# q and gate columns of the second pair of blocks by Strassen's algorithm, in a stage of their own

## Chip, cores, metric

One Trainium2 chip, one core. The time is the device time of one execution in microseconds (us), as a median of runs; beside it stands one profiled execution with its trace. TensorE (PE) multiplies, VectorE (DVE), ScalarE (ACT) and GpSimd (POOL) do the rest, SyncE (SP) issues most of the DMAs.

## The reference

One layer of a hybrid decoder on a prompt of 2048 tokens and 8 x 4 sample tokens (32 rows), width 1024:

```
h = rmsnorm(x); z = h @ w_in
hq, hf, hi, hg, sq, sk, sv, ga, gb = split(z)   # 512, 512, 512, 512, 512, 128, 128, 1024, 1024 columns
y_a = (rmsnorm(gated linear recurrence of hq, f(hf), hi) * silu(hg)) @ w_up_a
y_b = (sliding-window attention of rotary(sq), rotary(sk), sv, with sinks) @ w_up_b
m = sigmoid(ga) * y_a + sigmoid(gb) * y_b
x = x + m @ w_o
x = x + square(relu(rmsnorm(x) @ w_ff1)) @ w_ff2       # inner width 4096
y = rmsnorm(x)
```

The new state of the recurrence and the last window of keys and values are outputs as well.

## The kernel before

The prompt is cut into four blocks of 512 tokens (`bi` 0 to 3); the 32 sample rows join the last, which has T = 544. Two blocks make a pair (`sb` 0 and 1). A pair goes through its two blocks one after the other, up to the output projection `w_o`, and then both together through the MLP. Matrix products of float32 data are made of three passes in fp32r: each operand is split into a high part (ACT cast) and a low part (DVE subtraction), and high x high, high x low and low x high are added up in PSUM (`split_out`, `split_in`, `split_w`).

In a block all activations lie transposed as two operands `hT` (k tiles 0 to 3 and 4 to 7; slots 0 and 1 of seven large SBUF slots `op(0)` to `op(6)`, which every stage reuses). The order in the program: value columns hi (`colN512`), the pending norms of the block before (`late`), q columns hq (`colT`, four tiles of 128 columns), attention columns sq and skv, the attention over four chunks (`swa_scores`, `swa_values`), hf, the levels of the recurrence with hg in between (`hgrn_levels`), the outputs of the recurrence (`hgrn_out`, `hgrn_tail`), then eight tiles of gate gb with w_up_b and eight of gate ga with w_up_a (`gate`), then `w_o`. In `gate` a tile of the gate (8 k x 3 matmuls) goes through tanh on ACT, the up-projection (4 k x 3) into another PSUM bank, and DVE multiplies them; for ga POOL adds the other branch, and the sum is split into `mT`. A tile of 512 tokens is one matmul wide, in the last block two (288 and 256, `segs`).

The MLP is Strassen's algorithm already, in Winograd's form with seven products. The two blocks of the pair are the two halves of the token axis (Th = 512 or 528 each), the k tiles 0 to 3 and 4 to 7 the two halves of the inner axis, and two column tiles of w_ff1 the two halves of the columns: tile n is paired with tile n + 16. Sums of activations (S1 to S4) are made once, sums of weights (T1 to T4) for each pair of tiles (`Wpair`); in the second pair of blocks the 528 tokens go in two chunks of 264. `Unit` makes the seven products of a pair and chunk: `a` the two that need only unsummed operands (B11 A11, B21 A12), `b` three (T2 S2, T1 S1, T3 S3), `c` two (T4 A22, B22 S4). Of each PSUM bank a copy is taken between products (`snap`). The first six or ten units run their `a` ahead. The results and their sums go to DRAM (`us`, seven stores per unit) and are the operands of the second product (`f2`), which gathers its result in `yacc` in SBUF. While it runs for the first pair, block 2's activations are normalised and transposed (`load_T_parts`); block 3's during block 2's `w_o`. Then `Fin` transposes `yacc` back, adds the residual, normalises and stores.

The program is unrolled, and the Tile framework's planner sets the order on each engine at build time: it takes what its own cost model says is ready, with program order as priority. So a matmul group later in the program runs earlier where another waits. Waits between engines are semaphores. Tiles of a pool take turns in `bufs` buffers; a pool that is opened after another is closed takes the same memory, and its tiles wait for the old tiles that they overlap (`reuse_waits="tile"`).

Of the kernel before, what the change touches and what calls it, by code (L numbers as in the profile page):

```python
# [7 lines left out]
F32 = mybir.dt.float32  # L8
# [8 lines left out]
P = 128  # L17
# [26 lines left out]
def tile_hybrid_step(  # L44
# [188 lines left out]

    def geometry(bi):
# [16 lines left out]
    def load_T_parts(bi, i, hT, xt, on_dve=False, sm=None, junk=None, hwf=None):  # L251
        kind, r0, nr, c = geometry(bi)[5][i]
        src = xs if kind == "s" else xp[bi * bt + c * P:bi * bt + (c + 1) * P, :]
        N = f"ab{bi}{c}"
        x = []

        def pre():
            x.append(xt())
            nc.sync.dma_start(x[0][0:nr, :], src)
            norm_pre(x[0], x[0], nr, N, on_dve, sm, junk and junk())  # L260

        def out(half, tp, wb):
            hw = (hwf or t2)(f"hw_{N}_{half}")[:, 0:512].rearrange("p (k t) -> p k t", k=4)[:, :, 0:nr]
            nc.vector.tensor_tensor(hw, tp, wb, ALU.mult)
            split_out(hT[half][:, 0, :, r0:r0 + nr], hT[half][:, 1, :, r0:r0 + nr], hw)

        return pre, lambda: norm_post(x[0], nr, n1c, N, out)

    wk_ctx = ExitStack()
    wk = wk_ctx.enter_context(tc.tile_pool(name="wk0", bufs=1, reuse_waits="tile"))  # L270
    hT_next = start_T(0)
    x_first = op(6, F32, "x_first")
    for i in range(ncb):
        for part in load_T_parts(0, i, hT_next, lambda: x_first[:, i * D:(i + 1) * D], on_dve=True):
            part()
# [26 lines left out]
    def w2_sums(i):  # L302
        tt = nc.vector.tensor_tensor
        r = {}
        for kh in range(2):
            for nh in range(2):
                r[kh, nh] = wk.tile([P, 512], F32, tag="ws", bufs=5, name=f"ws{i}{kh}{nh}")
                nc.sync.dma_start(r[kh, nh], w2[(kh * NP + i) * P:(kh * NP + i + 1) * P, nh * 512:(nh + 1) * 512])
        t3 = wk.tile([P, 512], F32, tag="ws", bufs=5, name=f"ws{i}t")
# [4 lines left out]
        for o, x in (("T3", t3), ("T1", r[0, 1]), ("T2", r[1, 1]), ("T4", r[1, 0])):  # L314
            nc.sync.dma_start(wT[o][i * P:(i + 1) * P, :], x)

    late = []
    x1 = [tc.dram_tile([geometry(bi)[2], D], F32, name=f"x1_{bi}") for bi in range(nblk)]
    for bi in range(nblk):
# [28 lines left out]
        s1W = W1[:, 2 * n4:2 * n4 + 8 * NS].rearrange("p (x h t) -> p x h t", x=2, h=HH)
        qS, kS, fS, aS = s0W[:, 0], s0W[:, 1], s1W[:, 0], s1W[:, 1]
        SV = op(4, F32, "SV_" + B)  # L350
        qT = SV[:, 0:4 * T].rearrange("p (g t) -> p g t", g=G)
        vN = SV[:, 4 * TM:4 * TM + 512 * ncb].rearrange("p (c e) -> p c e", e=512)
        if smp:
            vS = wk.tile([NS, 512], F32, tag="vS", name="vS")
# [28 lines left out]
        def colN(c0, name, fn):  # L383
# [7 lines left out]
        def colN512(c0, name, fn):  # L391
            rings = [mm_ps, mm_ps, hg_ps, hg_ps, sw_ps]
            ps = [rings[i](f"ps_{name}_{t[3]}") for i, t in enumerate(tiles)]
            gemm_NK(w_in, c0, [(p, t[1], t[2]) for p, t in zip(ps, tiles)], h_acts, name)
# [81 lines left out]
        colN512(C_HI, f"hi{B}", ev_v)  # L476
        while late:
            norm_post(*late.pop(0))

        for h in range(HH):  # L480
            colT(C_HQ, h, f"hq{B}{h}", ev_q)
        qkv = op(5, F32, "qkv_" + B)[:, 0:len(tiles) * 768].rearrange("p (c e) -> p c e", e=768)

        def ev_sq(ps, kind, c, nr):
            ti = c if kind == "p" else ncb
            nc.scalar.activation(
                qkv[0:nr, ti, 0:512].rearrange("p (g v d) -> p v g d", g=G, v=NKV),
                ps.rearrange("p (v g d) -> p v g d", g=G, v=NKV), AF.Copy, scale=HD ** -0.5)
# [5 lines left out]
        colN512(C_SQ, f"sq{B}", ev_sq)  # L494
        colN(C_SQ + 512, f"skv{B}", ev_skv)

# [171 lines left out]

        for h in range(HH):
            colT(C_HF, h, f"hf{B}{h}", ev_f)  # L670

# [10 lines left out]
        while gens:  # L682
            gens = [g for g in gens if next(g, None) is not None]
            if rnd in hg_at:
# [88 lines left out]

        b_acts = [(ob[:, 0, k, :], ob[:, 1, k, :]) for k in range(4)]
        pb = op(5, F32, "pb_" + B)[:, 0:KD * T].rearrange("p (k t) -> p k t", k=KD)

        def gate(c0, j, uu, acts, dst, z):
            js = slice((j % 2) * P, (j % 2 + 1) * P)
            gu = unit_rows(w_in, 0, KD, c0 + j * P, P, f"g{z}{B}{j}")
            for (t0, n) in segs:  # L780
                N = f"{z}{B}{j}_{t0}"
                o = dst(j, t0, n)
                ps = mm_ps("g" + N)
                gemm_T(ps, n, [(gu[0][:, k, :], gu[1][:, k, :]) for k in range(KD)], h_acts, t0)
                nc.scalar.activation(o, ps[:, 0:n], AF.Tanh, scale=0.5)
                ps = sw_ps("y" + N)
# [4 lines left out]
        for j in range(KD):  # L791
# [6 lines left out]
            if sb == 0 and j % 2 == 1:  # L798
                w2_sums(8 * bi + j // 2)
# [7 lines left out]
        for j in range(KD):  # L807
            if sb == 0 and j % 2 == 1:
                w2_sums(8 * bi + 4 + j // 2)
            if j % 2 == 0:  # L810
                ua = unit_rows(w_ua, 0, 4, j * P, 256, f"ua{B}{j}")
            for t0, n, o in gate(C_GA, j, ua, a_acts, lambda j, t0, n: t2(f"ta_{B}{j}_{t0}")[:, 0:n], "a"):
# [27 lines left out]
        tt = nc.vector.tensor_tensor  # L840
# [65 lines left out]
        if odd:  # L906
            rings = (sw_ps, sw_ps, hg_ps, hg_ps, mm_ps)
# [14 lines left out]
        else:  # L922
            ntl = geometry(bi + 1)[5]
            loads = [load_T_parts(bi + 1, i, hT_next, lambda i=i: t4(f"x_b{bi + 1}_{i}")) for i in range(len(ntl))]
            todo = []
            for i in range(len(ntl) + 1):
                if i < len(ntl):
                    todo.append(loads[i][0])
                if i > 0:
                    todo.append(loads[i - 1][1])  # L930
# [7 lines left out]
            for cg in range(2):  # L938
                rings = ((sw_ps, sw_ps, hg_ps, hg_ps), (mm_ps, mm_ps, sw_ps, sw_ps))[cg]
# [9 lines left out]
        chunks = [(0, Th)] if Th <= 512 else [(0, Th // 2), (Th // 2, Th // 2)]  # L949
# [4 lines left out]

        def prod(ps, wv, av, k0, t0, n, first, last=True):
            for k in range(4):
                wh, wl = wv[:, 0, k, k0:k0 + P], wv[:, 1, k, k0:k0 + P]
                ah, al = av[:, 0, k, t0:t0 + n], av[:, 1, k, t0:t0 + n]
# [387 lines left out]
```

## Time and profile before

| | |
|---|---|
| median of 3 runs | 2934.21 us (2930.34 to 2935.71) |
| profiled execution | 2930.84 us, span of its instructions 2929.1 us |
| granted TensorE clock, mean | 0.992 |
| PE busy | 2841.5 us, 97% |
| weight loads (PEld) busy | 2453.5 us, 84% |
| DVE / ACT / POOL busy | 1629.4 / 1136.1 / 215.0 us |
| HBM read / written | 334.07 / 107.64 MB |

Matmuls are pipelined, so their durations overlap: what one costs is read from how many a stretch holds, not from its mean duration. The pair 0 of blocks ends near 1399 us of the span, block 2 at 1770, block 3 at 2229, the first MLP product of the second pair at 2584.

### The profile page before, as it was taken

The page shows a single profiled execution, that of the slowest core. Times are in us where ns is not written, and L with a number is a line of the kernel's source. Part 1 is how long each engine was busy: PE and PEld are TensorE (multiplying, and loading weights), DVE is VectorE, ACT ScalarE, POOL GpSimd, SP SyncE. Part 2 cuts the span into 40 slices and gives each one's busy share as a digit, 9 for nine tenths or more (in the row PEclk, how much of TensorE's full clock was granted, in tenths as well). Part 3 has the DMA queues.
Part 4 walks back from the last instruction along what each step waited for, and adds up shares of the span by engine and source line. Part 5 has one row for each costly group of instructions (what it writes and reads, how often), then busy time and mean ns, then how long its engine had stood idle before and what let it go on. Part 6 is the DMA issues. An engine that isn't in the chain of part 4 may idle for free.

```text
span 2929.1 us, 49035 instructions
## 1 busy us (share of the span) xinstructions
PE 2841.5 (97%) x19967; PEld 2453.5 (84%) x19967; DVE 1629.4 (56%) x2559; ACT 1136.1 (39%) x2093; POOL 215.0 (7%) x360
## 2 busy tenths in 40 slices
PE   7999999999899999999999999999998999999998
PEld 6778877788778888887777888878997999999998
DVE  5674434734777674454456343275347777754446
ACT  3443334423433344442354233333234333344433
POOL 0110111101200000000111011100003000000001
PEclk9999999999999999999999999999999999999999
DMA  7746342145654465565422434212346454485553
GB/s 251 238 154 219 105 144 66 45 122 158 197 165 155 159 232 206 196 214 173 151 64 68 125 115 135 62 52 84 116 133 197 151 157 140 146 304 179 186 195 104
DMA packets 410539, 443.92 MB, mean 152 GB/s; under 512 B 22588, under 2 KB 290840, under 8 KB 410296
## 3 DMA queue, kind: packets, MB, share of 16 engines
q1 hardware_dynamic: 402160, 413.48, 44.0%
q0 software_dynamic: 5600, 18.70, 2.1%
q10 hardware_dynamic: 2552, 8.60, 0.8%
q8 instruction: 157, 2.57, 0.4%
q14 instruction: 70, 0.57, 0.1%
HBM read 334.07 MB, written 107.64 MB: 151 GB/s over the span
## 4 chain that ended last, share of the span: by engine, by line
PE 43%; DMA 3%; DVE 2%; ACT 1%; issue 1%; POOL 1%; SPq 0%; POOLq 0%; DVEq 0%; ACTq 0%
PE f L1180 3%; PE f L1179 3%; PE f L1181 3%; PE fB L959 2%; PE fB L961 2%; PE fB L960 2%; PE gab L169 1%; PE gab L170 1%; PE gab L168 1%; PE gbb L170 1%; PE gbb L169 1%; PE gbb L168 1%; PE fD L959 1%; PE fD L961 1%; PE fD L960 1%
## 5 line engine op out<-in xcount | busy, mean ns | idle before, releaser
L1179 PE MATMUL f<-f2S,hw2T 128*128 128x264 f32 (+1 forms) x576 | 183.7, 319 | 0.0
L1180 PE MATMUL f<-f2S,hw2T 128*128 128x264 f32 (+1 forms) x576 | 183.6, 319 | 0.0
L1181 PE MATMUL f<-f2S,lw2T 128*128 128x264 f32 (+1 forms) x576 | 183.5, 319 | 0.0
L155 DVE TENSOR_TENSOR lw2T<-lw2T,hw2T 128x1024 fp32r<-128x1024 f32 x64 | 78.1, 1224 | 106.0 <-ACT hw2T L154 105.5
L959 PE MATMUL fB<-S,w1T 128*128 128x264 f32 (+1 forms) x384 | 124.2, 325 | 7.3 <-DVE c L1027 3.7
L1180 PE MATMUL f<-f2A,h_w2B 128*128 128x264 f32 (+1 forms) x384 | 122.5, 319 | 1.4 <-DVE f2A L155 1.4
L961 PE MATMUL fB<-S,w1T 128*128 128x264 f32 (+1 forms) x384 | 123.4, 322 | 0.0
L1179 PE MATMUL f<-f2A,h_w2B 128*128 128x264 f32 (+1 forms) x384 | 122.6, 319 | 0.8 <-ACT f2A L154 0.8
L960 PE MATMUL fB<-S,w1T 128*128 128x264 f32 (+1 forms) x384 | 123.3, 322 | 0.0
L1181 PE MATMUL f<-f2A,l_w2B 128*128 128x264 f32 (+1 forms) x384 | 122.2, 319 | 0.0
L154 ACT CAST hw2T<-lw2T 128x1024 fp32r<-128x1024 f32 x64 | 67.3, 1052 | 126.6 <-DMA lw2T<-w_T 114.3
L1180 PEld LDWEIGHTS f<-f2S,hw2T 128*128 128x128 f32 x576 | 108.4, 188 | 7.4
L1179 PEld LDWEIGHTS f<-f2S,hw2T 128*128 128x128 f32 x576 | 108.4, 188 | 7.4
L1181 PEld LDWEIGHTS f<-f2S,lw2T 128*128 128x128 f32 x576 | 108.0, 188 | 7.5
L169 PE MATMUL gbb<-hT_b,h_gbb 128*128 128x512 f32 (+2 forms) x320 | 113.2, 354 | 0.0
L168 PE MATMUL gbb<-hT_b,h_gbb 128*128 128x512 f32 (+2 forms) x320 | 113.1, 353 | 0.0
L170 PE MATMUL gbb<-hT_b,l_gbb 128*128 128x512 f32 (+2 forms) x320 | 112.9, 353 | 0.0
L169 PE MATMUL gab<-hT_b,h_gab 128*128 128x512 f32 (+2 forms) x320 | 111.7, 349 | 0.0
L170 PE MATMUL gab<-hT_b,l_gab 128*128 128x512 f32 (+2 forms) x320 | 111.6, 349 | 0.0
L168 PE MATMUL gab<-hT_b,h_gab 128*128 128x512 f32 (+2 forms) x320 | 111.4, 348 | 0.0
L155 DVE TENSOR_TENSOR f2S<-f2S 128x1024 fp32r<-128x1024 f32 (+1 forms) x64 | 79.4, 1242 | 51.9 <-ACT f2S L154 50.3
L231 DVE TENSOR_TENSOR l_w2B<-rw2B,h_w2B 128x1024 fp32r<-128x1024 f32 x48 | 58.8, 1225 | 81.1 <-ACT h_w2B L230 74.7
(717 smaller groups left out, 8821.1 us busy)
## 6 DMA issues: line engine op xcount, KB each, us to landing
w1r<-w_ff SPq DMA_DIRECT2D x150, 256.0 KB
lw2T<-w_T SPq DMA_DIRECT2D x64, 512.0 KB
rw2B<-w_ff SPq DMA_DIRECT2D x48, 512.0 KB
u_S<-s SPq DMA_DIRECT2D x128, 132.0 KB
f2S<-u_S SPq DMA_DIRECT2D x32, 528.0 KB
ws<-w_ff SPq DMA_DIRECT2D x64, 256.0 KB
r_gbb<-w_in SPq DMA_DIRECT2D x32, 512.0 KB
r_gab<-w_in SPq DMA_DIRECT2D x32, 512.0 KB
```

Source lines behind the costliest of these rows:

```text
L154: nc.scalar.copy(hi, F(lo))
L155: nc.vector.tensor_tensor(lo, F(lo), F(hi), ALU.subtract)
L168: nc.tensor.matmul(ps[:, 0:n], wh, rh, start=(k == 0), stop=False)
L169: nc.tensor.matmul(ps[:, 0:n], wh, rl, start=False, stop=False)
L170: nc.tensor.matmul(ps[:, 0:n], wl, rh, start=False, stop=(k == nk - 1))
L231: nc.vector.tensor_tensor(dl, src, F(dh), ALU.subtract)
L959: nc.tensor.matmul(ps, wh, ah, start=(first and k == 0), stop=False, skip_group_check=not first)
L960: nc.tensor.matmul(ps, wh, al, start=False, stop=False, skip_group_check=not first)
L961: nc.tensor.matmul(ps, wl, ah, start=False, stop=(last and k == 3), skip_group_check=not first)
L1179: nc.tensor.matmul(ps, wh, ah, start=first, stop=False, skip_group_check=cont)
L1180: nc.tensor.matmul(ps, wh, al, start=False, stop=False, skip_group_check=cont)
L1181: nc.tensor.matmul(ps, wl, ah, start=False, stop=lastk, skip_group_check=cont)
```

## The change

For the second pair of blocks (`zs`, sb > 0) the columns hq, gb and ga leave the blocks: 4 + 8 + 8 = 20 column tiles (NZ) become 10 pairs of neighbouring tiles, and a stage ahead of block 2 makes them for both blocks at once with the same seven products (`strassen_T`, now a function shared with the MLP).

- During the first pair's second MLP product all nine token tiles of the second pair are normalised (`norm_tile`), not four; the raw result goes to DRAM (`hraw`) by POOL's queue, and block 2's half is split into `hT` (528 tokens: 512 and 16 sample rows).
- Between the pairs: attention columns skv and sq of block 2, stored to DRAM (`zqk`); the four raw quarters come back by POOL's queue into tiles of a pool `zq` (14 buffers, 6 per k); `op_sums` makes S1 to S4 and A22 from them in slots 2 to 6.
- The stage runs in a pool `zp` opened after `zq` is closed. `z_fin` takes tanh of the gates on ACT and stores to DRAM (`zd`) from ACT's queue, the q tiles from POOL's.
- Block 2 reads q, k, v and both blocks read q (`qW`) and the gates (`pb`, `ga`) back by POOL's queue. `gate` is left with the up-projection. hi moves behind the attention. Block 3's activations are reloaded from `hraw` (`reload`) during block 2's `w_o`.
- In the MLP tile 2n is paired with 2n + 1, so that two loads of 256 columns take the place of four of 128; the weight sums are made in the loaded tiles; T4 is split later (`late`); T3 and T4 have buffers of their own (`we`); the result tiles have 12 buffers per chunk, not 16; the seven stores of a unit go by POOL's queue, not SP's. w_ff2 is read in the permuted order.
- In the first pair `w_o` uses other PSUM rings, and the normalised rows go to DRAM through `t4` tiles.

```diff
+    class Wpair:
+        def done(u, name, raw):
+            v = (u.wt if name in ("T3", "T4") else wtile)(F32R, ...)
+            split_out(v[:, 0], v[:, 1], raw)
+        def early(u):
+            v = wtile(F32, f"w1r0_{u.N}").rearrange("p (s k c) -> p s k c", s=2, k=4)
+            for kh in range(2):
+                nc.sync.dma_start(v[:, kh], u.src(u.n, kh)[:, 0:P].rearrange("(k p) c -> p k c", p=P))
+                u.done(f"B{kh + 1}1", v[:, kh])
+        def rest(u):
+            for kh in range(2):
+                v = wtile(F32, f"w1r{kh + 1}_{u.N}").rearrange("p (k c) -> p k c", k=4)
+                nc.sync.dma_start(v, u.src(u.n, kh).rearrange("(k p) c -> p k c", p=P))
+                b += [v[:, :, 0:P], v[:, :, P:2 * P]]
...
+            tt(b11, b12, b11, ALU.subtract)
+            tt(b12, b22, b12, ALU.subtract)
+            u.done("B22", b22)
+            tt(b22, b22, b11, ALU.subtract)
+            tt(b21, b21, b22, ALU.subtract)
+            u.done("T2", b22)
+            u.done("T1", b11)
+            u.done("T3", b12)
...
+    def strassen_T(N, npairs, src, chunks, A, st, fin, ahead, wt, hook=None):
...
+        for i in range(ahead):
+            if i % nch == 0:
+                units[i].pair.early()
+            units[i].a(i < 4)
+        for i, u in enumerate(units):
+            if i % nch == 0:
+                u.pair.rest()
+            if i >= ahead:
+                u.a()
+            if i:
+                units[i - 1].c()
+            if i % nch == 0:
+                u.pair.late()
+            u.b()
+        units[-1].c()
...
+                if raw:
+                    nc.gpsimd.dma_start(hraw[b][oo][...], hw[:, :, s:s + n])
+                if oo == tgt:
+                    split_out(hT[half][:, 0, :, d:d + n], hT[half][:, 1, :, d:d + n], hw[:, :, s:s + n])
...
+    def op_sums(A, sl, a11, a12, a21, a22, s1, s2):
+        tt(s1, a21, a22, ALU.add)
+        tt(s2, s1, a11, ALU.subtract)
+        tt(a11, a11, a21, ALU.subtract)
+        tt(a12, a12, s2, ALU.subtract)
+        for n, x in (("S2", s2), ("S1", s1), ("S3", a11), ("A22", a22), ("S4", a12)):
+            split_out(sl(A[n], 0), sl(A[n], 1), x)
...
+        if zs and not odd:
+            colN(C_SQ + 512, f"skv{B}", st_skv)
+            colN512(C_SQ, f"sq{B}", st_sq)
+            for k in range(4):
+                z = {n: zq.tile([P, Th], F32, tag="zs", bufs=14, ...) for n in ("a11", "a12", "a21", "a22", "s1", "s2")}
+                for n, o, g in (("a21", 1, 0), ("a22", 1, 1), ("a11", 0, 0), ("a12", 0, 1)):
+                    nc.gpsimd.dma_start(z[n], hraw[sb][o][(4 * g + k) * P:(4 * g + k + 1) * P, :])
+                op_sums(A, lambda v, i: v[:, i, k], *(...))
+            zq_ctx.close()
+            with tc.tile_pool(name=f"zp{sb}", bufs=1, reuse_waits="tile") as zp:
+                def z_fin(u, blk, x, ps=None):
+                    if zi >= HH:
+                        nc.scalar.activation(x, x if ps is None else ps, AF.Tanh, scale=0.5)
+                    q = nc.scalar if zi >= HH else nc.gpsimd
+                    if o == 0:
+                        q.dma_start(zd[bi][rs, c0:min(c1, bt)], x[:, 0:min(c1, bt) - c0])
+                        if c1 > bt:
+                            q.dma_start(zd[bi + 1][rs, 0:c1 - bt], x[:, bt - c0:u.ln])
+                    else:
+                        q.dma_start(zd[bi + 1][rs, o2 + c0:o2 + c1], x)
+                def z_st(ln, name):
+                    return zp.tile([P, ln], F32, tag="st", bufs=(16 if len(chunks) == 1 else 15), name=name)
+                strassen_T(f"z{sb}", NZ // 2, z_src, chunks, A, z_st, z_fin, 6 if len(chunks) == 1 else 10, ...)
...
+            if not zs:
+                gu = unit_rows(w_in, 0, KD, c0 + j * P, P, f"g{z}{B}{j}")
-                ps = sw_ps("y" + N)
+                ps = (sw_ps, mm_ps)[(j + i) % 2 if zs else 0](f"y{z}{B}{j}_{t0}")
...
+                s1, s2, s3, s4 = u.st("s1"), u.st("s2"), u.c21, u.st("s4")
-                        nc.sync.dma_start(us[o][u.n // 4][...], x)
+                    nc.gpsimd.dma_start(us[o][u.n // 4][...], y_)
-                    return fp.tile([P, u.ln], F32, tag="st", bufs=16 * len(chunks), ...)
+                       lambda ln, name: fp.tile([P, ln], F32, tag="st", bufs=12 * len(chunks), name=name),
```

More of the change, by code (lines that the diff above doesn't have):

```diff
@@ L231, in split_out, with prod @@
         nc.vector.tensor_tensor(dl, src, F(dh), ALU.subtract)
+    def prod(ps, wv, av, k0, t0, n, first, last=True):
+        for k in range(4):
+            wh, wl = wv[:, 0, k, k0:k0 + P], wv[:, 1, k, k0:k0 + P]
+            ah, al = av[:, 0, k, t0:t0 + n], av[:, 1, k, t0:t0 + n]
+            nc.tensor.matmul(ps, wh, ah, start=(first and k == 0), stop=False, skip_group_check=not first)
+            nc.tensor.matmul(ps, wh, al, start=False, stop=False, skip_group_check=not first)
+            nc.tensor.matmul(ps, wl, ah, start=False, stop=(last and k == 3), skip_group_check=not first)
@@ new lines, in strassen_T @@
+    def strassen_T(N, npairs, src, chunks, A, st, fin, ahead, wt, hook=None):
+        ws = [Wpair(N, n, src, wt) for n in range(npairs)]
+        nch = len(chunks)
+        units = [Unit(i, ws[i // nch], *chunks[i % nch], A, st, fin) for i in range(npairs * nch)]
+        for i in range(ahead):
[12 more added lines that the diff above has]
+            u.b()
+            if hook is not None:
+                hook()
+        units[-1].c()
@@ L269, in tile_hybrid_step, with hw_w @@
+        return [pre, lambda: norm_post(x[0], nr, n1c, N, out)]
+    hT_next = [opT(0, g, "hT") for g in range(2)]
+    x_first = op(6, F32, "x_first")
     wk_ctx = ExitStack()
     wk = wk_ctx.enter_context(tc.tile_pool(name="wk0", bufs=1, reuse_waits="tile"))
[L271 to L274, printed above, removed]
+    def hw_w(name):
+        x = wtile(F32, name)
+        return x, lambda half: x[:, half * 512:(half + 1) * 512]
@@ new lines, in hw_t2, with z_ops @@
+    def hw_t2(name):
+        return None, lambda half: t2(f"{name}{half}")
+    def z_ops(b):
+        return {n: opT(b, slot, "z" + n) for n, slot in (("S1", 4), ("S2", 5), ("S3", 3), ("A22", 2), ("S4", 6))}
+    def op_sums(A, sl, a11, a12, a21, a22, s1, s2):
[5 more added lines that the diff above has]
+            split_out(sl(A[n], 0), sl(A[n], 1), x)
@@ L275, in tile_hybrid_step @@
+    for (o, c) in tiles_of(0)[:ncb]:
+        for part in norm_tile(0, (o, c), hT_next, lambda: x_first[:, c * D:(c + 1) * D], small, hw_t2, True, raw=False):
             part()
@@ L474, in ev_v, with qk_in, qk_out @@
             nc.scalar.copy(vS if kind == "s" else vN[:, c, :], ps)
[L476 to L482, printed above, removed]
+        def qk_in(ps):
+            return ps.rearrange("p (v g d) -> p v g d", g=G, v=NKV)
+        def qk_out(x):
+            return x.rearrange("p (g v d) -> p v g d", g=G, v=NKV)
@@ L953, in tile_hybrid_step @@
         us = {o: [tc.dram_tile([4 * P, Th], F32, name=f"u_{o}_{g}_{sb}") for g in range(KG)] for o in OPS}
[L955 to L958, printed above, removed]
-                nc.tensor.matmul(ps, wh, ah, start=(first and k == 0), stop=False, skip_group_check=not first)
-                nc.tensor.matmul(ps, wh, al, start=False, stop=False, skip_group_check=not first)
-                nc.tensor.matmul(ps, wl, ah, start=False, stop=(last and k == 3), skip_group_check=not first)
         with tc.tile_pool(name=f"f1_{sb}", bufs=1, reuse_waits="tile") as fp:
@@ L1215, in tile_hybrid_step @@
                                 evac(si, j, t0, ln, banks[j][ci])
-                    if not last and 1 <= si <= ncb and g in (1, 2):
-                        loads[si - 1][g - 1]()
+                    if not last and si >= 1 and todo:
+                        todo.pop(0)()
             nj = op(6, F32, f"nj{sb}")
```

418 lines of the change are left out of this document (238 added, 180 removed).

## The prediction

> **What bounds the kernel now.** I read the page first: the span, busy times, and the chain that ended last.
>
> ```profile
> span 2929.1 us, 49035 instructions
> PE 2841.5 (97%) x19967; PEld 2453.5 (84%) x19967; DVE 1629.4 (56%) x2559; ACT 1136.1 (39%) x2093; POOL 215.0 (7%) x360
> PE 43%; DMA 3%; DVE 2%; ACT 1%; issue 1%; POOL 1%; SPq 0%; POOLq 0%; DVEq 0%; ACTq 0%
> ```
>
> TensorE works in 97% of the span and leads the chain; no other engine passes 56%. So time comes off where TensorE's work shrinks, and goes back on where it then waits. Next the busy time by stretches, cut at the work concerned: gates of block 2, gates of block 3, the first MLP product of the second pair (Strassen already, in chunks of 264 tokens), the passage from the first pair to block 2, the start of that product in the first and in the second pair, and the recurrence's outputs in blocks 2 and 3. Columns: stretch, length, then busy us and instructions of PE, weight loads, VectorE, ScalarE, GpSimd; granted clock; DMA.
>
> ```profile
> 1600.00:1720.00 120.00, 120.00 (x532) 99.34 (x531) 43.21 (x48) 39.50 (x51) 10.03 (x9) 1.00 0.38 112
> 2035.00:2170.00 135.00, 135.00 (x1075) 135.00 (x1074) 47.05 (x74) 38.33 (x65) 10.79 (x14) 1.00 0.34 100
> 2300.00:2575.00 275.00, 274.11 (x2229) 271.80 (x2228) 199.93 (x432) 99.05 (x214) 0.00 (x0) 1.00 0.48 152
> 1399.00:1429.00 30.00, 27.83 (x137) 21.56 (x135) 19.66 (x27) 13.05 (x28) 7.88 (x19) 1.00 0.59 189
> 757.00:810.00 53.00, 45.35 (x194) 36.58 (x193) 42.59 (x64) 24.50 (x40) 10.00 (x15) 0.94 0.66 212
> 2229.00:2300.00 71.00, 58.99 (x440) 57.26 (x439) 53.19 (x96) 29.23 (x56) 9.81 (x14) 0.93 0.64 200
> 1570.00:1600.00 30.00, 28.06 (x363) 24.78 (x362) 17.14 (x36) 18.68 (x54) 8.00 (x12) 1.00 0.16 44
> 1980.00:2035.00 55.00, 51.59 (x511) 42.39 (x509) 33.85 (x60) 20.04 (x68) 6.78 (x10) 0.94 0.32 92
> ```
>
> The reader is to see three rates of TensorE, all without idle time: 120/532 = 0.2256 us for a matmul of 512 columns, 135/1075 = 0.1256 for the 288/256 columns of block 3, 275/2229 = 0.1234 for 264. Time goes by columns, with some 6% more per column at 264 than at 512. And a Strassen stage pays at its start: from 2229 to 2300 TensorE stood 71 - 59.0 = 12.0 us and had a clock of 0.93, another 0.07 x 71 = 5.0; the first pair's start 7.7 and 0.06 x 53 = 3.2.
>
> **The matmuls, minus 21.6 us.** Gone from the blocks: 20 column tiles (4 of q, 8 and 8 of the gates) x 8 k x 3 passes = 480 matmuls of 512 in block 2, 480 x 0.2256 = 108.3 us, and 960 in block 3, 960 x 0.1256 = 120.6. New: 10 pairs x 7 products x 4 k x 3 passes x 2 chunks = 1680 of 264, x 0.1234 = 207.3. All of it lay on TensorE's path: 228.9 - 207.3 = 21.6 saved, not the eighth of 228.9 (28.6), since the narrow matmuls cost more per column.
>
> The weight loads speak against that saving: there are 1680 instead of 1440, and at 264 columns they are in flight for 271.8 of 275 us. If they set the spacing, 240 more at 0.1234 would be 30 us more instead. The rows all but exclude it: at 512 columns, with the same weight load, a matmul takes 1.83 times as long, so the columns set it.
>
> The Trainium skill (TensorE: Matmul & The Clock Gate, "Back-to-back issue gap") has a rule of that kind: weight load and stream set the spacing together, about 81 ns at 128 columns and 131 at 512. Interpolated, an estimate from that page, the old matmuls would take 480 x 131 + 960 x 100 = 159 us and the new 1680 x 99 = 166, a loss of 7 where the rows give a gain of 21.6. The trace disagrees with the page's rates for this kernel's own shapes (226 and 123 ns).
>
> **Start of the new stage, plus 7 (0 to 17).** Before it come block 2's k/v and query columns, then ten units of two products that need only the plain activations. All other operands are built by VectorE from raw activations, loaded by GpSimd into tiles that lie where the first pair's accumulator (yacc) was; its last reads are the final transposes. Later the stage's result tiles (st) lie where these raw tiles were, and the first copy out of PSUM needs one. From the timeline (start, length, instruction): the last product of the first pair, its last transposes, its last normalised rows. Then groups by line (busy us, mean ns) and POOL's DMA issues (count, size, us to landing):
>
> ```profile
> 1398.43 0.40 PE L1181 MATMUL f<-f2A,lw2T 128*128 128x512 f32 x1
> 1413.75 0.66 PE L1151 MATMUL fy<-ident,yacc 128*128 128x128 f32 x4 [0.42 <-DVE fx L1153]
> 1420.47 1.41 DVE L1163 SCALAR_TENSOR_TENSOR fx<-fx,fr,nfb 128x512 f32<-128x512 f32 x2 [2.03 <-POOL fr L200]
> L231 DVE TENSOR_TENSOR S<-sw_1p,S 128x512 fp32r<-128x512 f32 x8 | 5.3, 688 | 6.0 <-ACT S L230 6.0
> L231 DVE TENSOR_TENSOR l_hib<-r_hib,h_hib 128x1024 fp32r<-128x1024 f32 x4 | 4.9, 1220 | 0.6 <-ACT h_hib L230 0.6
> h2T<-h2w_b POOLq DMA_DIRECT2D x16, 256.0 KB, 3.4
> S<-dS POOLq DMA_DIRECT2D x6, 512.0 KB, 4.9
> ```
>
> TensorE's cover from 1398.4: transposes (some 3 us), 96 narrow matmuls (12.1) and 96 wide ones (21.7), then six products into free PSUM banks, 6 x 12 x 0.1234 = 8.9: to about 1444. VectorE's side: loads from 1414, landed by 1418 (3.4 to 4.9); 4 x 9 operations of 528 columns at 688 ns = 24.8; the first pair's output norms (to 1421.9) and four weight splits of 1220 lie between, some 8: to about 1451. Two k fit in the 14 raw tiles, so half of the loads wait for release; some st tiles come free before the end. I take 5 us idle, and by the 5.0 per 12.0 above 2 for the clock. Ends: hidden (0), or as the dearer of the two MLP starts (17.0); the cheaper, 10.9, is the nearer row, but had no 46 us of other work ahead of it.
>
> **End of the stage and lost covers, plus 3 (0 to 17).** Behind the stage block 2 starts anew from DRAM (rotary needs qkv, in the slot of S2, free five products before the end, 7 us; landing 4.9), with the value columns (96 x 0.2256 = 21.7) as filler: 1. In the recurrence's output loops gate matmuls stood in for idle time (groups by line from 1570 to 1600 and from 1980 to 2035, one of three passes each):
>
> ```profile
> L168 PE MATMUL gbb<-hT_b,h_gbb 128*128 128x512 f32 x8 | 3.5, 438 | 0.0
> L168 PE MATMUL gbb<-hT_b,h_gbb 128*128 128x288 f32 (+1 forms) x20 | 6.4, 321 | 0.0
> ```
>
> Three passes of each: 24 x 0.2256 = 5.4 us in block 2, 60 x 0.1256 = 7.5 in block 3. If nothing takes their place, that is 13, and some 4 more at the new passage. But the up-projection of the same branch (96 x 0.2256 = 21.7; 192 x 0.1256 = 24.1) no longer waits for a gate on TensorE and can fill in: 2.
>
> **At nothing, with their cover.** In the stage (rows of the groups by line; the store issue by its source line: shortest, median, longest ns) VectorE has per unit 3 additions of 426 ns and half of eleven 688s: 5.1 of 84 x 0.1234 = 10.4 us. ScalarE: 3 copies of 376, 4 tanh of 425, 3.5 casts of 616 and on average 5 stores to issue: 1.1 + 1.7 + 2.2 + 1.6 = 6.6.
>
> ```profile
> L1025 ACT COPY c<-fB 128x264 f32<-128x264 f32 x6 | 2.3, 376 | 6.1 <-PE fB L961 6.1
> L1060 ACT ACTIVATE c<-c 128x264 f32<-128x264 f32 x3 | 1.3, 425 | 0.1
> L230 ACT CAST w1B<-w1r 128x512 fp32r<-128x512 f32 x9 | 5.4, 616 | 0.0
> L1040 DVE TENSOR_TENSOR p<-fC,p 128x264 f32<-128x264 f32 x22 | 9.4, 427 | 3.4 <-PE fC L961 3.3
> L903 ACTq DMA_DIRECT2D x<-y_b x16: 326/326/368, 386.8 to 2230.5; - x16
> L890 POOL DMA_DIRECT2D dA<-h_b x4 | 3.2, 796 | 2.3 <-DVE h_b L870 2.3
> L116 POOL DMA_DIRECT2D cf<-c_f x1 | 0.8, 750 | 0.5 <-issue 0.5
> ```
>
> The norms and 40 transposes of block 3 move from block 2's output projection into the first pair's second MLP product; as many leave as arrive, and both stretches are TensorE's. SyncE's queue loses the 40 old column loads of 512 KB, gains 20 and ten small ones, and hands 336 stores of MLP results to GpSimd: 7 x 0.75 = 5.3 us per 10.4 us unit there, in a stage where GpSimd had 0.00 busy. Behind them on that queue wait only the next stores; the second product reads the last of them some 30 us later. Without that cover the result buffers (24 instead of 32) would run dry and hold the copy out of PSUM. The raw activations (20 writes, 16 loads) and the reloads of gates, q and k/v (23) have a whole phase between issue and use; the exception, the first loads of the stage, is priced above. Neighbouring w1 tiles halve the number of loads in a stretch at 0.48 DMA share, where PE is 99.7% busy: nothing. In the first pair the output projection takes other PSUM rings and its rows go out through bigger buffers; the wait that this touches there is small, so 0, ends minus and plus 2.6:
>
> ```profile
> PE tp_fb L225 <- DVE h2w_b L862: 2.6, 3, 1.6
> ```
>
> The new order at the two MLP starts could move their idle time by a few us either way (12.0 in the second); I take 0, ends minus 5 and plus 5.
>
> **Sum.** -21.6 + 7 + 3 = -11.6. The profiled execution took 2930.84, so 2919.2; the median of the three runs, 2934.21, lies 3.4 higher, so I say 2922.
>
> **Rivals.** (1) The start is hidden: DRAM loads land early, st tiles come free in time. For it: 46 us of cover. Against: VectorE is 66% busy there already. -21.6 + 1: 2914. (2) Start as the MLP's (17) and half of the lost cover shows (6): +1 on balance, 2936, no change. For it: the two Strassen starts in this trace lost 10.9 and 17.0. (3) Slower, by one mechanism: the copy of c12. The next product into the same bank must wait for it, and only one product lies between, 12 x 0.1234 = 1.5 us. In the MLP this wait is small (waits from 2300 to 2575: total us, times, longest),
>
> ```profile
> PE fB L959 <- ACT c L1025: 0.5, 1, 0.5
> ```
>
> with ScalarE at 99/275 = 36%. Here it is at 6.6/10.4 = 63%, and tanhs (425) and store issues (326) of the unit before stand ahead in its queue. With the 10 us lost elsewhere, it decides from (11.6 + 5.9)/20 = 0.9 us per unit on; at 1.2 it gives -11.6 + 24, 2947. (4) GpSimd's issues slow down beside a busy VectorE. At 200/275 = 73% busy a locked-out issue would take 0.75/0.27 = 2.8 us, seven of them 19.4 against 10.4: 32 units x 9 = 290 us more, some 3220. The rows speak against it: 796 ns in a stretch of heavy VectorE work, 750 at the kernel's idle start. The Trainium skill (SBUF — State Buffer, "SBUF: two separate sides") has this lock for perf-mode operations and advises against GpSimd-issued DMAs beside them; by that rule the moved stores are the change's worst part. The trace shows 6% at most.
>
> **Chances.** Below 0.2% (5.9 us) this kernel's runs can't tell a change. Forecast, 6 to 18 us less: 0.50. (1) 0.17. (2) 0.17. (3) 0.13. (4) 0.02. A spacing set by weight loads, 2930.8 + 30 + 10 + 3.4 = 2974: 0.01. Faster takes the first two: 0.67; same (2); slower the rest, 0.16. The likeliest case alone spans 2916 to 2928; with (1) and the ends of its terms, with (2) and the mild half of (3), 2907 to 2941.
>
> **What would show it.** Matmuls of 264 in the new stage at 0.1234 us; the 16 gate tiles' matmuls gone from blocks 2 and 3, where TensorE goes from the recurrence straight to the up-projections without idle time; between the first pair's last product and the first product with S2, one wait of some 5 us for a result tile or a raw tile and a dip of the granted clock; the wait of the second product for c12's copy below 0.2 us per unit. Wrong if that wait is the largest one, if the outputs of the recurrence show idle time over 5 us per block, or if GpSimd's store issues take over 1 us each.

## Result and the profile after

The changed kernel takes 2915.41 us (median of 10 runs, 2911.64 to 2927.66), the kernel before 2934.95 beside it: ratio 0.9946, 95% interval 0.993 to 0.9962, or 16 us less (so the means of the runs; the medians differ by 19.5). The profiled execution took 2911.64 us, the fastest of the ten. From its page, the first lines and the shares of the chain that ended last:

```profile
span 2908.8 us, 50329 instructions
PE 2814.7 (97%) x20207; PEld 2446.7 (84%) x20207; DVE 1705.9 (59%) x2739; ACT 1161.3 (40%) x2191; POOL 451.0 (16%) x791
PE 41%; DMA 3%; DVE 2%; issue 2%; POOL 1%; ACT 1%; SPq 0%; POOLq 0%; DVEq 0%; ACTq 0%
```

TensorE still sets the end; it has 240 matmuls more and 26.8 us less work. Where the 20.3 us between the two spans lie is read from the stretches, each cut at the same event: the blocks of the first pair (to its first MLP product), that product, the second product (to its last matmul), from there to block 3's `w_o`, and the second pair's second product with the end of the program (block 3's `w_o` and the second pair's first product lie between the last two and are not shown). Columns as in the prediction. Before:

```profile
0.00:757.80 757.80, 728.74 (x5255) 588.23 (x5255) 400.10 (x625) 295.07 (x589) 81.28 (x129) 1.00 0.48 150
757.80:1078.10 320.30, 307.77 (x1331) 251.86 (x1329) 234.53 (x361) 118.68 (x201) 9.81 (x14) 0.98 0.53 175
1078.10:1398.80 320.70, 318.34 (x1427) 262.13 (x1427) 165.72 (x164) 138.94 (x158) 5.46 (x15) 1.00 0.59 204
1398.80:2170.40 771.60, 753.90 (x6226) 640.15 (x6225) 363.40 (x625) 290.89 (x659) 84.11 (x138) 0.99 0.33 96
2575.70:2929.10 353.40, 341.06 (x2804) 338.34 (x2804) 181.06 (x207) 140.49 (x184) 12.21 (x31) 0.99 0.56 191
```

After, the same events:

```profile
0.00:751.90 751.90, 726.92 (x5255) 587.24 (x5255) 400.42 (x625) 295.77 (x589) 81.57 (x129) 1.00 0.48 151
751.90:1065.10 313.20, 305.02 (x1331) 250.25 (x1330) 238.11 (x362) 121.09 (x201) 67.14 (x120) 0.99 0.53 179
1065.10:1392.30 327.20, 322.60 (x1467) 266.15 (x1466) 170.38 (x176) 149.52 (x176) 30.86 (x58) 1.00 0.64 220
1392.30:2143.40 751.10, 726.62 (x6426) 630.94 (x6425) 431.59 (x788) 303.12 (x737) 116.42 (x196) 0.99 0.41 130
2548.60:2908.80 360.20, 341.44 (x2805) 338.30 (x2804) 177.56 (x204) 138.25 (x182) 15.66 (x38) 0.98 0.55 186
```

The changes are -5.9, -7.1, +6.5, -20.5 and +6.8 us, and -0.1 in what lies between. So the stretch with the new stage brings 20.5; the first pair and the end of the program, which were put at nothing, move by as much as 7 each, in both directions, and nearly cancel. Inside the 20.5, TensorE's work shrank by 27.3 (the matmuls' 21.6 by the prediction's sum, and 40 transposes that moved into the stretch above, where PE rose by 4.3), and its idle time grew from 17.7 to 24.5.

The start of the stage, the stage in steady flow, and the outputs of the recurrence in blocks 2 and 3:

```profile
1435.00:1475.00 40.00, 37.68 (x292) 37.07 (x293) 35.05 (x62) 22.65 (x49) 3.76 (x7) 0.96 0.57 188
1475.00:1640.00 165.00, 164.64 (x1340) 163.10 (x1339) 82.25 (x148) 67.70 (x146) 6.98 (x13) 1.00 0.35 110
1760.00:1808.00 48.00, 42.44 (x419) 36.95 (x419) 27.11 (x49) 19.59 (x53) 7.71 (x12) 0.96 0.36 122
2056.00:2110.00 54.00, 51.01 (x476) 42.88 (x471) 38.07 (x69) 18.08 (x61) 7.86 (x12) 0.97 0.48 154
```

A matmul of 264 columns takes 165.00/1340 = 0.1231 us. The start has two waits, from the timeline (in brackets the idle time before the matmul, and what ended it):

```profile
1435.57 0.39 PE L238 MATMUL fB_z<-hT,w1B_z 128*128 128x264 f32 x1 [2.41 <-ACT zqk_b L672]
1450.93 0.39 PE L238 MATMUL fC_z<-hT,w1B_z 128*128 128x264 f32 x1 [1.74 <-DVE p_z L315]
```

The first product waits for a PSUM bank that ScalarE has not yet emptied of block 2's query columns; the later one for an addition (L315) that stands on VectorE behind all the activation sums. The two waits are 4.15 us; with a clock of 0.96 over 40 us (0.04 x 40 = 1.6) the start costs 5.8.

### The profile page after: what moved, and what is told of

Its sections match the earlier page's. It is cut to its first block, busy times and chain, and to the rows that moved or that the text cites. A ratio compares the mean times of both kernels' runs of the same rounds, so it can differ in the third digit from the quotient of the medians.

```text
span 2908.8 us, 50329 instructions
## 1 busy us (share of the span) xinstructions
PE 2814.7 (97%) x20207; PEld 2446.7 (84%) x20207; DVE 1705.9 (59%) x2739; ACT 1161.3 (40%) x2191; POOL 451.0 (16%) x791
## 4 chain that ended last, share of the span: by engine, by line
PE 41%; DMA 3%; DVE 2%; issue 2%; POOL 1%; ACT 1%; SPq 0%; POOLq 0%; DVEq 0%; ACTq 0%
PE f L1349 3%; PE f L1350 3%; PE f L1351 3%; PE fB_f L238 2%; PE fB_f L240 2%; PE fB_f L239 2%; PE fB_z L238 1%; PE fB_z L240 1%; PE fB_z L239 1%; PE fD_f L240 1%; PE fD_f L238 1%; PE fD_f L239 1%; PE wob L191 1%; PE wob L193 1%; PE wob L192 1%
## 5 line engine op out<-in xcount | busy, mean ns | idle before, releaser
L238 PE MATMUL fB_f<-S,w1T_f 128*128 128x264 f32 (+1 forms) x384 | 123.0, 321 | 3.1 <-ACT c_f L300 2.6
L239 PE MATMUL fB_f<-S,w1T_f 128*128 128x264 f32 (+1 forms) x384 | 122.3, 319 | 0.0
L240 PE MATMUL fB_f<-S,w1T_f 128*128 128x264 f32 (+1 forms) x384 | 122.2, 319 | 0.0
L230 ACT CAST w1T_f<-w1r_f 128x512 fp32r<-128x512 f32 x128 | 77.2, 619 | 69.2 <-PE fB_f L240 28.9
L231 DVE TENSOR_TENSOR w1T_f<-w1r_f,w1T_f 128x512 fp32r<-128x512 f32 x128 | 87.4, 688 | 23.6 <-ACT w1T_f L230 23.4
L1254 POOL DMA_DIRECT2D u_S<-s_f x144 | 77.7, 541 | 114.0 <-DVE s_f L1249 95.9
L1254 POOL DMA_DIRECT2D u_A<-c_f x104 | 56.2, 540 | 235.3 <-DVE c_f L1238 229.7
L154 ACT CAST f2S<-f2S 128x1024 fp32r<-128x1024 f32 (+1 forms) x64 | 67.9, 1064 | 53.5 <-DMA f2S<-u_S 51.1
L300 ACT COPY c_f<-fB_f 128x264 f32<-128x264 f32 (+1 forms) x80 | 36.1, 451 | 126.4 <-PE fB_f L240 117.3
```

Source lines behind the costliest of these rows:

```text
L154: nc.scalar.copy(hi, F(lo))
L230: nc.scalar.copy(dh, src)
L231: nc.vector.tensor_tensor(dl, src, F(dh), ALU.subtract)
L238: nc.tensor.matmul(ps, wh, ah, start=(first and k == 0), stop=False, skip_group_check=not first)
L239: nc.tensor.matmul(ps, wh, al, start=False, stop=False, skip_group_check=not first)
L240: nc.tensor.matmul(ps, wl, ah, start=False, stop=(last and k == 3), skip_group_check=not first)
```

## Experiments

Ratios are to the kernel before, run beside it, with their 95% interval in brackets; 0.0010 is 2.9 us. Each edit is made in the changed kernel, called after here, unless another base is named. The code is cut to the lines that matter (`...`).

**The shared edits alone, and with the store queue undone: e1_shared, e8_shared_sp, e2_stores_sp.**

```diff
-        zs = sb > 0
+        zs = False                      # e1_shared, e8_shared_sp (with norms and pools to match)
...
-                    nc.gpsimd.dma_start(us[o][u.n // 4]...   # stores of the first MLP product
+                    nc.sync.dma_start(us[o][u.n // 4]...     # e2_stores_sp, e8_shared_sp
```

> All the edits that both pairs of blocks share, without the new stage: q and gates of blocks 2 and 3 are computed in the blocks, as before. Main theory (the gain is TensorE's columns, -21.6 us, less what the new stage's start and lost covers cost): this kernel stands where the kernel before does, 2935 within 5, or a few us better by the re-planned first pair (-6.5 in the trace of after), and a few worse by GpSimd's closing drain (9.6 us in after, 2.1 in before); its 1440 matmuls of q and gates are back (480 at 0.2256 and 960 at 0.1256 us). Rival (the shared edits, among them neighbouring tiles, in-place sums and the moved norms, bring the gain): within 5 us of after, 2915.

> After, with the stores of the MLP's first product issued by SyncE's queue again instead of GpSimd's. Theory (GpSimd's closing drain grows with the DMAs that it issued and ends the span): drain back towards 2 to 5 us, its end no longer the last thing, 2 to 4 us faster than after. Rival 1 (moving the stores relieved SyncE, whose weight loads now come late): 2 to 10 us slower, with waits of TensorE for weight tiles in both MLPs. Rival 2 (the drain's length has another cause): as after within 1 us, drain still 9 to 10 us.

> The shared edits without the stage (as e1_shared), and the MLP's result stores on SyncE's queue (as e2_stores_sp). Theory (the stores on GpSimd's queue cost some 15 us by themselves, in the MLPs and at the end, and the other shared edits give as much back): the two effects add, e1_shared's 2931 less 15, about 2914 to 2918, 0.995 of before. Rival (the stores cost that much only in the kernel with the stage, whose own GpSimd DMAs lengthen the queue and the closing drain): 2929 within 3, as before.

Measured: e1_shared 2931.3 us, 1.0004 [0.9993, 1.0015]; e8_shared_sp 2917.6, 0.9946 [0.9932, 0.996]; e2_stores_sp 2897.81, 0.9896 [0.988, 0.9911]. With after they are four kernels, with and without the stage, with the stores by GpSimd and by SyncE, and two effects that add up fit them: the stage brings 0.0058 (17 us, with GpSimd's stores) or 0.0050 (15 us, with SyncE's), and the move of 336 stores to GpSimd costs the same 0.0058 (without the stage) or 0.0050 (with it), 15 to 17 us, some five times the 2 to 4 that I had expected from the drain alone. A third pair of kernels, e3_ring and e7_sp_ring below, puts the move at 0.0056. The other shared edits give 0.0054 (16 us) back; in e1_shared the stores' price hid that, so its main expectation came true by two effects that cancelled. e2_stores_sp's stretches, to be held against those of after:

```profile
1061.80:1387.30 325.50, 323.75 (x1467) 267.49 (x1466) 171.65 (x177) 149.43 (x176) 27.68 (x52) 0.99 0.65 221
1387.30:2139.60 752.30, 727.17 (x6425) 631.58 (x6424) 432.51 (x787) 303.35 (x737) 117.13 (x196) 0.99 0.42 130
2546.30:2897.10 350.80, 339.31 (x2794) 336.76 (x2792) 177.05 (x202) 136.82 (x180) 12.19 (x31) 0.99 0.56 190
```

The stage's stretch stays (752.3 against 751.1); the end falls from 360.2 to 350.8. GpSimd's queue is closed at the end of the program by DRAIN instructions; in before, after and e2_stores_sp (shortest, median and longest in ns, then the first and the last start):

```profile
L1335 POOLq DRAIN  x3: 40/102/2057, 2923.1 to 2928.8; - x3
```
```profile
L1502 POOLq DRAIN  x3: 40/102/9647, 2898.4 to 2908.6; - x3
```
```profile
L1502 POOLq DRAIN  x3: 40/93/3528, 2891.5 to 2896.8; - x3
```

In after the drain runs from 2898.4 to 2908.05, when SyncE had finished at 2904.3; in e2_stores_sp it ends before SyncE's first DRAIN (2896.3). Another place is the passage from the first MLP product to the second. ScalarE in the first pair, after:

```profile
1065.17 1.05 ACT L154 CAST f2S<-f2S 128x1024 fp32r<-128x1024 f32 x1 [3.42 <-DMA f2S<-u_S]
1067.03 1.04 ACT L154 CAST f2S<-f2S 128x1024 fp32r<-128x1024 f32 x1 [0.81 <-DMA f2S<-u_S]
1067.98 0.58 ACT L300 COPY c_f<-fB_f 128x512 f32<-128x512 f32 x1
```

and in e2_stores_sp:

```profile
1061.98 0.59 ACT L300 COPY c_f<-fB_f 128x512 f32<-128x512 f32 x1 [0.48 <-PE fB_f L240]
1064.03 1.05 ACT L154 CAST f2S<-f2S 128x1024 fp32r<-128x1024 f32 x1 [1.46 <-DMA f2S<-u_S]
```

In after the copy out of PSUM stands behind casts that wait for reloaded results, and TensorE waits 2.2 us for it. In e2_stores_sp the copy comes first: the planner put the two in another order when the stores changed their queue, so this price is one of the kernel as it was planned, not of the queue alone. Across all kernels this wait is 2.2 to 4.1 us where the first pair's stores go by GpSimd, and absent where they go by SyncE.

**Which pair's stores: e12_sp_first, e13_sp_second.**

```diff
-                    nc.gpsimd.dma_start(us[o]...
+                    (nc.gpsimd if zs else nc.sync).dma_start(us[o]...   # e12: first pair by SyncE
+                    (nc.sync if zs else nc.gpsimd).dma_start(us[o]...   # e13: second pair by SyncE
```

> After, with the result stores on SyncE's queue in the first pair's MLP only; the second pair's stay on GpSimd's. The theory puts the 15 us between after and e2_stores_sp at three places: first pair's MLP (its wait of 2.2 to 4.0 us for c_f at the passage to the second product, with the clock behind it), the same passage in the second pair (some 3 us), and GpSimd's closing drain (4.6 us of tail). Then half is gained here: 6 to 9 us faster than after, tail still 2 to 4 us longer than before's 9.6, the first passage without a wait. Rival (only the end of the program counts, the backlog at the drain): within 3 us of after.

> The complement of e12_sp_first: the result stores on SyncE's queue in the second pair's MLP only, on GpSimd's in the first pair's. With e12_sp_first no faster than after, the theory left is that the second pair's stores cost nearly all: the closing drain (tail 14.1 instead of 9.3) and the passage to its second product. Then this kernel stands with e2_stores_sp: 0.9896 to 0.991 of before, tail below 10, the first pair's wait of 2 to 4 us at its passage back. Rival (the cost is spread, or is no single place): half way, 0.992 to 0.993; or as after, 0.9946, if only both together help.

Measured: e12_sp_first 2912.82, 0.9942 [0.9927, 0.9957], 1 us less than after; e13_sp_second 2909.42, 0.9929 [0.9909, 0.9948], 5 less. In the traces the places follow the queue: e12 has no wait at the first passage but a drain of 9892 ns and 3.5 us of waits at the second passage; e13 a wait of 3.7 at the first, a drain of 3363 and 1.3 at the second. In time the two do not add up to the 15 us of both, though with 6 us of uncertainty on each difference they could. e12's 6 to 9 us did not come. Its rival, that only the end counts, fits its own time, but then e13 would have stood with e2_stores_sp's 0.9896 to 0.991, and it stands half way, as e13's rival says. The stretches place the cost better than the times do. First pair's second product and second pair's second product with the end, e12_sp_first and then e13_sp_second:

```profile
1068.80:1393.70 324.90, 322.54 (x1467) 266.11 (x1466) 171.81 (x177) 149.47 (x176) 27.61 (x52) 1.00 0.65 222
2550.60:2911.00 360.40, 341.28 (x2806) 338.31 (x2804) 178.03 (x204) 138.21 (x182) 15.94 (x38) 0.98 0.54 186
1068.80:1400.30 331.50, 325.44 (x1467) 268.07 (x1466) 170.47 (x176) 149.21 (x176) 30.86 (x58) 0.99 0.64 218
2563.80:2913.70 349.90, 339.25 (x2793) 336.70 (x2792) 176.64 (x202) 137.47 (x180) 12.22 (x31) 0.99 0.56 190
```

With the stage, the end takes 358 to 360 us where the second pair's stores go by GpSimd (after, e12_sp_first, e3_ring, e5_q_back) and 350 to 351 where they go by SyncE (e2_stores_sp, e13_sp_second, e7_sp_ring): 7 to 10 us, about half of it behind TensorE's last matmul (13.8 in after, 9.0 in e2_stores_sp). The first pair's second product takes 327 to 334 us where the first pair's stores go by GpSimd (after, e3_ring, e5_q_back, e13_sp_second) and 325 where they go by SyncE (e2_stores_sp, e7_sp_ring, e12_sp_first): 2 to 9 us. Without the stage (e1_shared against e8_shared_sp) the two differences are 3 and 5 us. So the cost lies in both pairs. That the times of e12 and e13 don't show it may be noise of the size named below: their profiled executions spent 758 us on the first pair's blocks, where after's spent 752.

**The start of the stage: e3_ring, e7_sp_ring, e10_sums_pool, e11_start.** In e3_ring the query columns before the stage use other PSUM banks, in turn (a ring); e7_sp_ring is the same on e2_stores_sp; e10 and e11 are e7_sp_ring with activation sums on GpSimd.

```diff
-            colN512(C_SQ, f"sq{B}", st_sq)
+            colN512(C_SQ, f"sq{B}", st_sq, rings=(sw_ps, sw_ps, tp_ps, tp_ps))   # e3, e7, e10, e11
...
-        tt(s1, a21, a22, ALU.add)                          # and three more per k
+        nc.gpsimd.tensor_tensor(s1, a21, a22, ALU.add)     # e10: every k; e11: k = 1 to 3, loads ahead
```

> After, with the second pair's query columns in the PSUM rings that the stage's first products don't use. Theory (the 2.4 us wait of the first B11 x A11 for ScalarE's copies out of PSUM, and the half clock of 3.4 us behind it, are the start's price): both go, 2 to 4 us faster than after. Rival (that wait only stands in for VectorE's operand sums, which end at 1449.9): TensorE waits as long at the first fC or at the first product with S2, and the time is after's within 1 us.

> e2_stores_sp with e3_ring's PSUM rings, VectorE doing all sums as in after. If e2_stores_sp's gain is the stores' and the ring only moves the start's wait to VectorE's chain (as e3_ring's trace showed): 0.989 to 0.991 of before. If e2_stores_sp was a lucky placing and the stores don't matter: 0.994 to 0.996, as e3_ring and after.

> e2_stores_sp with e3_ring's PSUM rings, and the four activation sums of each k on GpSimd instead of VectorE. e3_ring's trace moved the start's wait to VectorE, which runs without a gap from the landing of the raw activations (1419.9) to 1449 and only then adds fC. Theory (VectorE's chain sets the start): 16 x 0.70 = 11 us of that chain go, both waits (2.4 and 1.7 in after, 6.7 in e3_ring) fall below 1 us in total, 3 to 5 us faster than e2_stores_sp: 2893 to 2895. Rival (the landing of the raw loads sets it, or GpSimd at over 1.1 us a sum is the new bound: 16 x 1.2 = 19 us): a wait of 3 to 7 us stays before the first product with S2, 2897 to 2900.

> e10_sums_pool mended: there the raw loads of k = 1 to 3 stood behind the sums on GpSimd's queue in order (the last was issued at 1445, TensorE waited 7.3 and 11.0 us). Here the loads of three k go out ahead of all sums, k = 0 is summed by VectorE, k = 1 to 3 by GpSimd (12 x 1.33 = 16 us). Theory (VectorE's chain of sums and splits sets the start): it ends some 8 us earlier than 1449, both waits of the start below 1 us in total, 3 to 5 us faster than e2_stores_sp: ratio 0.988 to 0.9885 of before. Rival (landing of the raw activations, 4 to 7 us behind the issue, or the ring of 14 tiles sets it): a wait of 3 us or more stays, as e2_stores_sp, 0.9896, or slower.

Measured: e3_ring 2919.68, 0.9965 [0.9954, 0.9977]; e7_sp_ring 2901.78, 0.9909 [0.9891, 0.9928]; e10_sums_pool 2918.17, 0.9953 [0.9939, 0.9968]; e11_start 2910.92, 0.9935 [0.992, 0.9951]. The ring brings nothing: e3_ring is 6 us slower than after and e7_sp_ring 4 slower than e2_stores_sp, with 6 and 7 us of uncertainty. It takes the first wait away and lengthens the second, e3_ring's timeline:

```profile
1448.76 0.59 PE L238 MATMUL fC_z<-hT,w1B_z 128*128 128x264 f32 x1 [6.73 <-DVE p_z L315]
```

So the rival of e3_ring holds in the waits: VectorE's queue sets the start, as the prediction's sum of some 8 + 24.8 us had it (to about 1451; the last split ends near 1450 in after). Taking load off VectorE then failed: against e7_sp_ring's 0.9909, e10_sums_pool is 13 us slower and e11_start 8. In e11_start, VectorE's subtractions, two beside GpSimd's sums and one after their end, and two of GpSimd's sums:

```profile
1439.15 1.83 DVE L231 TENSOR_TENSOR zS<-zs2b,zS 128x528 fp32r<-128x528 f32 x1
1440.90 1.83 DVE L231 TENSOR_TENSOR zS<-zs1b,zS 128x528 fp32r<-128x528 f32 x1
1454.92 0.70 DVE L231 TENSOR_TENSOR zS<-zs2b,zS 128x528 fp32r<-128x528 f32 x1
```
```profile
1437.05 1.63 POOL L444 TENSOR_TENSOR za11b<-za11b,za21b 128x528 f32<-128x528 f32 x1
1438.64 1.77 POOL L445 TENSOR_TENSOR za12b<-za12b,zs2b 128x528 f32<-128x528 f32 x1
```

The same subtraction takes 1.83 us beside GpSimd and 0.70 alone; GpSimd's sum takes 1.33 alone (e10_sums_pool's first) and 1.6 to 1.8 here. Two operations of 0.62 (VectorE's pitch alone) and 1.3 one after the other would be 1.9: they take turns. The Trainium skill (SBUF — State Buffer, "SBUF: two separate sides") calls the port that the two share an exclusive lock, which a VectorE operation with two SBUF inputs takes part in; the trace agrees. TensorE waited 13.7 us for the addition behind this chain, in place of 6.7 in e3_ring and 5.6 in e7_sp_ring. The sharing is not all of it: GpSimd's twelve sums in e11_start begin at 1433.4, behind the last loads on its queue, which wait for free tiles, and at 1.33 each they would have ended near 1449 too, no earlier than VectorE's own chain in e3_ring. In e10_sums_pool the loads stood behind the sums: waits of 7.3 and 11.0.

**The size of a matmul: e4_chunks3.**

```diff
-                strassen_T(f"z{sb}", NZ // 2, z_src, chunks, A,
+                strassen_T(f"z{sb}", NZ // 2, z_src, [(i * 176, 176) for i in range(3)], A,
```

> After, with the stage's tokens in three chunks of 176 instead of two of 264: 2520 matmuls in place of 1680, the same columns. Columns theory (a matmul takes its columns' time, 0.1231 x 176/264 = 0.082 us): the stage stays near 207 us, the time within 6 us of after. Rival (a weight load and its issue set the spacing; the transposes of 128 columns stand 0.109 apart): 2520 x 0.11 = 277 us, about 65 us slower. In between, a spacing of a fixed part and a part by columns, as from 0.2256 at 512 and 0.1231 at 264 (0.014 + 0.000413 per column): 0.087, 12 us slower.

Measured: 3243.14 us, 1.1057 [1.1033, 1.1081], worse than any of the expectations. Second and last of the first product's twelve matmuls, and two stretches of the stage:

```profile
1434.74 0.28 PE L239 MATMUL fB_z<-hT,w1B_z 128*128 128x176 f32 x1
...
1435.86 0.27 PE L240 MATMUL fB_z<-hT,w1B_z 128*128 128x176 f32 x1
```
```profile
1500.00:1700.00 200.00, 199.25 (x923) 197.29 (x923) 41.98 (x88) 30.82 (x76) 10.29 (x19) 0.50 0.14 42
1700.00:1900.00 200.00, 199.35 (x934) 199.12 (x934) 38.22 (x73) 40.54 (x105) 0.00 (x0) 0.50 0.13 39
```

At full clock ten spacings take 1.12 us, 0.112 each and not 0.082: the rival's floor is there, and would have cost some 75 us (2520 x 0.112 - 1680 x 0.1231). That it is the weight load's, as the rival says, fits 197 us of weight loads in 200, but no run tries it apart. The rest is the clock: it fell to 0.50 behind the start's waits, as in after, where it is back after 3.4 us; here it stays there for the whole stage, some 545 us, at 200/923 = 0.217 us per matmul.

**Query columns back in the blocks: e5_q_back.**

```diff
-    NZ = HH + 2 * KD
+    NZ = 2 * KD
...
+            for h in range(HH):
+                colT(C_HQ, h, f"hq{B}{h}", ev_q)
```

> After, with the four query tiles back in the blocks (behind the attention, as before) and only the 16 gate tiles in the stage: 2 of 10 pairs fewer. Columns theory: a fifth of the 21.6 us is given back, 4.3 slower than after. Rival (the block loses idle-time cover by the move, so that a tile that stays is worth more than its columns): equal to after or faster, with less idle time of TensorE at the recurrences. Either way the stage is 336 matmuls shorter at 0.123 us each.

Measured: 2923.44, 0.9978 [0.9967, 0.9989], 9 us slower than after with 6 us of uncertainty. The columns' 4.3 lie within it; that a tile that stays as cover is worth more than its columns (equal to after or faster) is not borne out.

**The stage for both pairs: e9_both_sp.**

```diff
-        zs = sb > 0
+        zs = True                       # on e2_stores_sp; first pair: one chunk of 512, all 8 tiles normalised first
```

> e2_stores_sp with the stage for the first pair of blocks as well (one chunk of 512 tokens there; q and gates leave blocks 0 and 1, 960 matmuls of 512 become 840). Columns theory: 960 x 0.2256 - 840 x 0.2256 = 27 us less work, less a start that can't hide behind a pair before it (all 8 token tiles are normalised before the first product: 10 to 25 us more at the kernel's start): 2885 to 2900. Rival (the start costs more than the columns bring): above 2905.

Measured: 2943.66, 1.0038 [1.0024, 1.0052], 42 us slower than e2_stores_sp: the rival. Up to the first pair's MLP the kernel takes 792.8 us, TensorE idle for 70.8 of them at a clock of 0.96; e2_stores_sp takes 751.3, with 23.8 idle at 1.00. TensorE's waits up to 760 us, the largest:

```profile
PE ps_sqb L191 <- ACT h_sqb L230: 17.4, 1, 17.4
PE tp_ab L225 <- DVE x_first L216: 13.3, 3, 7.7
```

With no pair ahead of it, the start of the stage is not covered: 42 and the columns' 27, which are a sum and were not measured here, make 69 us, not the 10 to 25 that I expected.

## Why the prediction came out right, step by step

The forecast was 2922 us, 11.6 less; the ratio of 0.9946 on the 2934.21 shown gives 2918, 16 less, inside the likeliest case (2916 to 2928; 6 to 18 less). The bare median of 2915.41 lies just below it, inside the whole range of 2907 to 2941 and nearer to rival (1)'s 2914, whose mechanism did not occur. The main terms were right. That the total was right as well is luck: two terms of some 16 us each, which the prediction put at nothing, had opposite signs and cancelled.

- **Matmuls, -21.6.** As said: 0.1231 us per matmul instead of 0.1234, and the gate tiles are gone from the blocks. The floor under the spacing, to whose effect I gave 1 in 100, is real but lies at 0.112 in e4_chunks3; 264 columns stand 10% above it. At 176 columns, there, the columns no longer set the time.
- **Start, +7, and end with lost covers, +3.** TensorE's idle time between the pairs and block 3's `w_o` grew by 6.8 us (17.7 to 24.5), not 10. The start took 5.8, by other waits than I named: a PSUM bank behind ScalarE and an addition behind VectorE's sums, not a result tile; that VectorE is what sets it was right. Lost cover shows in block 2's outputs: 48.0 - 42.44 = 5.6 us against 1.9 before, over the 5 us that I had given as a sign of being wrong (before's figure is for 30 us; the 48 us up to the same point hold 2.2); in block 3 they have 3.0 against 3.4. The stage's own worth, -21.6 + 6.8 = -14.8 with the trace's idle time, agrees with the 15 and 17 us of the experiments; my -11.6 was 3 to 5 too small a gain.
- **At nothing: the stores on GpSimd.** This step failed. Rival (4) priced a slowed issue, and that did not come: 144 stores took 541 ns on average.

```profile
L1254 POOL DMA_DIRECT2D u_S<-s_f x144 | 77.7, 541 | 114.0 <-DVE s_f L1249 95.9 <-DVE s_f L1251 7.2 <-DVE s_f L1252 3.9
```

  But the step "behind them on that queue wait only the next stores; the second product reads the last of them some 30 us later" left out the first tiles that are read back at the passage, with ScalarE's copies in line behind them, and the closing drain. By the four kernels it is 15 to 17 us; by the stretches, with the stage, 7 to 10 at the end of the program and 2 to 9 in the first pair's second product.
- **At nothing: the first pair, 0 with 2.6, and the MLP starts, 0 with 5.** Also wrong, as a term put at nothing. Without GpSimd's stores the shared edits gain 16 us; in e8_shared_sp's trace 9.4 of them lie in the first pair's first MLP product (320.3 to 310.9). In before TensorE waited there, up to 895 us, for

```profile
PE tp_fb L225 <- ACT h_b L218: 3.6, 1, 3.6
PE fB L959 <- DVE c L1027: 3.5, 1, 3.5
PE fB L961 <- DVE w1B L231: 3.0, 1, 3.0
PE fB L959 <- ACT w1B L230: 1.1, 1, 1.1
PE fB L959 <- ACT c L1025: 0.7, 1, 0.7
```

  of which e8_shared_sp keeps the first (3.6) and 2.0 of the third. I had read these waits as the start's and let them stand. Which of the edits (paired loads, sums in place, T4 split later) removes them was not tried apart. The 4 to 6 us in the blocks ahead of it are no finding but noise: kernels with the same instructions there (after, e12_sp_first, e13_sp_second) take 751.9, 758.0 and 757.7 us to that point.
- **Rivals.** (1) gave 2914, and the start was not hidden; (2) fell with a start of 5.8 in place of 17. (3) fell: VectorE and ScalarE were busy for 50% and 41% of the steady stage, and all that TensorE waited for in those 165 us is

```profile
PE fB_z L238 <- DVE c_z L302: 0.4, 1, 0.4
```

The best version is the change with the MLP's stores left on SyncE: 2897.81 us, 1.0% under before and 0.5% under after; with the other PSUM banks as well it stands at 0.9909, which is no better.

## What to carry to other kernels

A DMA moved to an idle queue isn't free just because its issue is: follow the data to its first reader, look at what stands behind that reader on its engine, and at how the queue is closed at the end. Where an edit has several parts that touch stages outside its aim, price these by their own waits in the trace; here they moved as much time as the aim did. And sums that bind VectorE are not halved by giving some to GpSimd: in e11_start the two took turns, and TensorE waited longer.

## What the runs showed of the hardware that was not expected

- GpSimd's closing drain grew with what it had issued in the second pair: 2.06 us in before, 3.5 in e2_stores_sp, 3.4 in e13_sp_second (stores of the first pair on its queue), 9.9 in e12_sp_first (of the second), 9.6 in after (of both); 5.7 in e1_shared, which has the same stores and no stage. Why it keeps growing with stores that landed long before, no run here shows.
- A matmul of 176 columns has a spacing of 0.112 us, and a stream of them did not win the full clock back: some 545 us at 0.50 with TensorE listed as busy for 199 of 200 us. The Trainium skill (TensorE: Matmul & The Clock Gate, "What's actually happening") has the gate open after one busy window of about 3.4 us; with 264 columns the trace agrees (back after 3.4 us), with 176 it does not.
- VectorE and GpSimd took turns in e11_start where both worked on two SBUF inputs: 0.70 becomes 1.83 us, 1.33 becomes 1.6 to 1.8.
